# Rotary queries laid out on all 128 rows, with zeros in the other head's half, in one buffer

## The chip, the cores and the metric

The kernel runs on one NeuronCore of a Trainium2 chip, as one program. The metric is the time of one execution on the device in microseconds (us); the runs of a kernel are summed up by their median. A profile is one further execution with the hardware profiler on.

## The reference

The program computes one block of a diffusion transformer (adaptive layer norm, neighbourhood attention, convolutional feed-forward network) on 256 tokens of width 2048, and behind it a hybrid layer that adds an mLSTM branch and a branch of latent attention. All is in float32. The change lies in the latent attention, which is this:

```python
H_B = 16; D_NOPE = 128; D_ROPE = 64; D_HQK = D_NOPE + D_ROPE
...
    q_b = jnp.einsum('bsr,rn->bsn', rms_norm_2(c_q, q_lat_g), w_uq).reshape(b_sz, s_len, H_B, D_HQK)
    kv_b = jnp.einsum('bsr,rn->bsn', rms_norm_2(c_kv, kv_lat_g), w_ukv).reshape(b_sz, s_len, H_B, D_NOPE + D_VB)
    k_nope, v_b = jnp.split(kv_b, [D_NOPE], axis=-1)
    k_b = jnp.concatenate([k_nope, jnp.broadcast_to(k_r[:, :, None, :], (b_sz, s_len, H_B, D_ROPE))], axis=-1)
    q_b = rms_norm_2(q_b, q_norm_g)
    k_b = rms_norm_2(k_b, k_norm_g)
    q_b = jnp.concatenate([q_b[..., :D_NOPE], apply_rope(q_b[..., D_NOPE:], cos, sin)], axis=-1)
    k_b = jnp.concatenate([k_b[..., :D_NOPE], apply_rope(k_b[..., D_NOPE:], cos, sin)], axis=-1)
    o_b = causal_attention(q_b, k_b, v_b).reshape(b_sz, s_len, D_B)
```

So a head's query has 192 numbers, 128 plain ones and 64 that are rotated by the position; the score is the product over all 192, and 256 queries meet 256 keys under a causal mask.

## The kernel before, in words

Float32 precision comes from pairs: every operand is split into a high part (rounded to the matmul's input type, by ScalarE, ACT) and a low part (the rest, by VectorE, DVE), and a product is made of three matmuls, high by high, high by low and low by high (`mm3`), or of two where the two parts of one operand lie side by side. Weights come from HBM in tiles `raw` of 1 MB, are split into `whi` and `wlo`, and are multiplied at once. A Python planner writes the instructions out: it keeps an estimate of each engine's time, a heap of things that become due (`spawn`, `at`, `yield`), rings of buffers (`Ring`; `get` waits, in the planner, until a buffer is back), and the eight banks of PSUM. The order on each engine is the order in which the planner emits; each engine then works its list in order.

The latent attention comes after the mLSTM branch, 2 heads (a group g) at a time, 8 groups. `mla_begin` sets up the buffers. `mla_units(g)` multiplies the latents (`latkv`, `latq`) with the group's weights; `mla_q` and `mla_k` normalise and rotate the result, turn it with TensorE (PE) transposes (from `bsq`, `bx`, `bkt`) and split it: `bq` and `bk` hold the 128 plain rows, `bqr` and `bkr` the rotary ones. In `bqr` and `bkr` the 64 rotary numbers of the group's first head are rows 0 to 63, those of the second head rows 64 to 127. `mla_attn(h)` makes the scores of head h: for each block of 128 queries (t = 0, 1) three matmuls of `bk,bq` over 128 rows and three of `bkr,bqr` over the head's 64 rows, into the same bank; 128 keys for t = 0 and 256 for t = 1. So a head has 12 score matmuls, and within them the number of rows goes 128, 64, 128, 64. Behind them come mask and softmax (tile `bp`), three transposes of `bp`, the split into `bpt`, and the product with the values (`bpt,bv`, 6 matmuls over 128 rows: three with 256 columns, three with 128). Between these PE has the matmuls of the gate projection `mla_z` (`h,whi` and `h,wlo`, with 512 and 256 columns) and the next group's `latkv` and `latq`. In the rows every matmul stands under the line of `mm` (L257), a transpose under L266, and all DVE and ACT work under L152, so that names tell them apart.

Of the kernel before, what the change touches and what calls it, by code (L numbers as in the profile page):

```python
# [13 lines left out]
F32R = mybir.dt.float32r  # L14
# [520 lines left out]
def col(c):  # L535
    return slice(c * 128, (c + 1) * 128)
# [18 lines left out]
class Model(Kern):  # L555
# [1189 lines left out]
    def mla_begin(self):  # L1745
        self.need(lambda: self.y_stashed == 4)
        self.L.pop("ya")
        self.R.pop("y")
        self.sgring = Ring(self, self.L.push("sgb"), "sgb", [128, 256], F32, 8)
        p = self.R.push("obf")  # L1750
        self.obF = p.tile([128, KD, 256], F32, name="obF")
        p = self.R.push("mla")
        self.lat = {n: p.tile([128, 2, 4, 256], F32R, name="lat" + n) for n in ("q", "kv")}
        self.lat_ready = set()
        self.qring = Ring(self, p, "bq", [128, 2, 512], F32R, 2)
        self.kring = Ring(self, p, "bk", [128, 2, 512], F32R, 2)
        self.qrring = Ring(self, p, "bqr", [128, 2, 256], F32R, 2)
        self.krring = Ring(self, p, "bkr", [128, 2, 256], F32R, 2)
        self.v_left = {}
        self.vring = Ring(self, p, "bv", [128, 2, 2, 256], F32R, 2)  # L1760
        self.zring = Ring(self, p, "bz", [128, 256], F32, 6)
        self.sqring = Ring(self, p, "bsq", [128, 2, 2, 192], F32, 2)
        self.ktring = Ring(self, p, "bkt", [128, 768], F32, 1)
        self.xring = Ring(self, p, "bx", [128, 2, 2, 64], F32, 3)
        self.pring = Ring(self, p, "bp", [128, 384], F32, 2)
        self.ptring = Ring(self, p, "bpt", [128, 2, 384], F32R, 2)
        self.q, self.k, self.v, self.qr, self.kr, self.rq, self.zb = {}, {}, {}, {}, {}, {}, {}
        self.b_ready, self.ob_ready = {}, set()
        self.need(lambda: self.kr_ready)
# [10 lines left out]
    def mla_q(self, g, banks):  # L1780


        self.rq[g] = self.ccring.get()
        c = self.rq[g][0]
        x, xi = self.sqring.get()
        y, yi = self.xring.get()
        z, zi = self.xring.get()
        for t in range(2):
            o = banks[t].t[:, 0:384].rearrange("p (h c) -> p h c", h=2)
            for j in range(2):  # L1790
                self.act(y.rearrange("p t h c -> p (t h c)")[:, 0:192], o[:, j], AF.Square,
                         accum_out=c[:, 12 + 2 * t + j:13 + 2 * t + j])
            self.A.copy(out=x[:, t], in_=o)
            banks[t].free()
        yield
        yield from self.rotate(y, x[:, :, :, 128:192], z, "q", 2)
        yield from self.rsqrt(c[:, 0:4], c[:, 12:16], 192, c[:, 4:12], sign=-1.0)
        self.xring.put(zi)
        yield
        b, b2 = self.bank(), self.bank()  # L1800
        for t in range(2):
            for j in range(2):
                self.tr(b.t[:, 256 * j + 128 * t:256 * j + 128 * t + 128], x[:, t, j, 0:128])
            self.tr(b2.t[:, col(t)], y[:, t].rearrange("p h c -> p (h c)"))
        self.sqring.put(xi)
        self.xring.put(yi)
        yield 0.2
        d, di = self.qring.get()
        r, ri = self.qrring.get()
        self.q[g], self.qr[g] = (d, di), (r, ri)  # L1810
        self.act(d[:, 0], b.t, AF.Copy, scale=self.bqn)
        self.A.copy(out=r[:, 0], in_=b2.t[:, 0:256])
        yield
        self.stt(d[:, 1], b.t, self.bqn, d[:, 0].bitcast(F32), ALU.mult, ALU.subtract)
        b.free()
        self.V.tensor_sub(out=r[:, 1], in0=b2.t[:, 0:256], in1=r[:, 0])
        b2.free()
        self.mla_go(g)

# [90 lines left out]

    def mla_attn(self, h):
        g, j = h // 2, h % 2
        half, cj = slice(64 * j, 64 * j + 64), 256 * j
        q, k, qr, kr, r = self.q[g][0], self.k[g][0], self.qr[g][0], self.kr[g][0], self.rq[g][0]
        b = self.bank()
        for t in range(2):
            o = b.t[:, 0:128] if t == 0 else b.t[:, 128:384]
            qs, ks = slice(cj + 128 * t, cj + 128 * t + 128), slice(cj, cj + 128 * (t + 1))
            self.mm3(o, q[:, 0, qs], q[:, 1, qs], k[:, 0, ks], k[:, 1, ks], True, False)
            qs, ks = col(t), slice(0, 128 * (t + 1))  # L1920
            self.mm3(o, qr[half, 0, qs], qr[half, 1, qs], kr[half, 0, ks], kr[half, 1, ks], False, True)
        self.b_left[g] = self.b_left.get(g, 2) - 1
        if not self.b_left[g]:
            self.qring.put(self.q.pop(g)[1])
            self.kring.put(self.k.pop(g)[1])
            self.qrring.put(self.qr.pop(g)[1])
            self.krring.put(self.kr.pop(g)[1])
        yield 0.2
        p, pi = self.pring.get()
        s, si = self.ccring.get()  # L1930
        tri = self.con("tri0")
        V = self.V
        for t in range(2):
            c = slice(0, 128) if t == 0 else slice(128, 384)

            V.tensor_tensor_reduce(out=b.t[:, c], in0=b.t[:, c], in1=tri[:, 128:256] if t == 0 else tri,
                                   scale=r[:, 2 * t + j:2 * t + j + 1], scalar=3e38, op0=ALU.add, op1=ALU.min,
                                   accum_out=s[:, t:t + 1])
        yield
        for t in range(2):  # L1940
            c = slice(0, 128) if t == 0 else slice(128, 384)
            self.act(p[:, c], b.t[:, c], AF.Exp, scale=-1.0, bias=s[:, t:t + 1], accum_out=s[:, 2 + t:3 + t])
        b.free()
        self.rq_left[g] = self.rq_left.get(g, 2) - 1
        if not self.rq_left[g]:
            self.ccring.put(self.rq.pop(g)[1])
        yield
        V.reciprocal(out=s[:, 4:6], in_=s[:, 2:4])
        for t in range(2):
            c = slice(0, 128) if t == 0 else slice(128, 384)  # L1950
            V.tensor_scalar(out=p[:, c], in0=p[:, c], scalar1=s[:, 4 + t:5 + t], scalar2=None, op0=ALU.mult)
        self.ccring.put(si)
        yield
        b = self.bank()
        for c in range(3):
            self.tr(b.t[:, col(c)], p[:, col(c)])
        self.pring.put(pi)
        yield 0.2
        pt, pti = self.ptring.get()
        self.A.copy(out=pt[:, 0], in_=b.t[:, 0:384])  # L1960
        yield
        self.V.tensor_sub(out=pt[:, 1], in0=b.t[:, 0:384], in1=pt[:, 0])
        b.free()
        yield
        self.need(lambda: h in self.zb)
        b = self.bank()
        v = self.v[g][0]
        c = col(j)
        self.mm3(b.t[:, 0:256], v[:, 0, 0, c], v[:, 1, 0, c], pt[:, 0, 0:256], pt[:, 1, 0:256], True, False)
        self.mm3(b.t[:, 128:256], v[:, 0, 1, c], v[:, 1, 1, c], pt[:, 0, 256:384], pt[:, 1, 256:384], False, True)  # L1970
        self.ptring.put(pti)
        self.v_left[g] = self.v_left.get(g, 2) - 1
        if not self.v_left[g]:
            self.vring.put(self.v.pop(g)[1])
        yield 0.2
        z, zi = self.zb.pop(h)
        self.tt(self.obF[:, h], b.t[:, 0:256], z, ALU.mult)
        b.free()
        self.zring.put(zi)
        self.ob_ready.add(h)  # L1980
# [222 lines left out]
```

## Time and profile before

| | |
|---|---|
| median of 3 runs | 2597.22 us (2588.12, 2597.22, 2597.39) |
| the profiled execution | 2589.92 us, of which span 2588.1 us |
| PE busy | 2530.4 us, 98% of the span |
| DVE, ACT busy | 71%, 55% of the span |
| mean granted PE clock | 0.993 of full speed |
| latent attention, first and last score matmul | 2138.6 us, 2337.7 us |

The span runs from the first to the last instruction of the core. The granted clock is the share of TensorE's full 2.4 GHz that was let through; it has two levels in the trace, 1.0 and 0.5.

### The profile page before, as it was taken

To read this page: it belongs to the slowest core of one execution; us is meant where nothing else is said; L and a number is where in the kernel's file an instruction comes from. 1 tells how busy PE (TensorE), PEld (TensorE's weight loads), DVE (VectorE), ACT (ScalarE), POOL (GpSimd) and SP (SyncE) were. 2 spreads that over 40 slices of the span, in tenths; PEclk is the share of its full clock that TensorE was granted. 3 is DMA by queue.
4 is the path that set the end of the run, shared out by engine and by line. 5 is a ranking of instruction groups with operands and counts; after the bars stand their busy time and mean duration, and the time that the engine had idled before them with its cause. 6 is when DMAs were issued, how large, how long until landed. Compare 5 with 4: busy or idle time off the path is not lost.

```text
span 2588.1 us, 37928 instructions
## 1 busy us (share of the span) xinstructions
PE 2530.4 (98%) x14694; PEld 2198.0 (85%) x14694; DVE 1842.5 (71%) x2995; ACT 1418.7 (55%) x2585; POOL 241.4 (9%) x263
## 2 busy tenths in 40 slices
PE   4999999999989999999999999999999999999999
PEld 2788888888978888888888888888888888888888
DVE  7988777776688887887555567677665576677664
ACT  5664444445555555555444557666554467776442
POOL 5422111211110000000000140000000000000000
PEclk8999999999999999999999999999999999999999
DMA  7887677665656666665565654554555643345554
GB/s 271 293 257 227 218 221 218 212 219 166 215 183 226 232 219 231 228 227 199 202 210 207 204 172 174 179 188 155 179 203 188 212 171 135 123 143 204 199 208 155
DMA packets 82533, 522.19 MB, mean 202 GB/s; under 512 B 9233, under 2 KB 15377, under 8 KB 23857
## 3 DMA queue, kind: packets, MB, share of 16 engines
q1 hardware_dynamic: 76656, 501.88, 55.6%
q0 software_dynamic: 5696, 17.90, 3.9%
q8 instruction: 115, 1.88, 0.3%
q14 instruction: 66, 0.53, 0.1%
HBM read 511.35 MB, written 8.39 MB: 201 GB/s over the span
## 4 chain that ended last, share of the span: by engine, by line
PE 92%; DVE 4%; ACT 2%; DMA 1%; issue 1%; SPq 0%; DVEq 0%; ACTq 0%
PE bank L257 90%; PE bank L266 2%; DVE wlo L152 2%; DVE acc L152 1%; ACT whi L152 0%; DMA raw<-in_na_w_qkv_dram 0%; ACT L150 0%; DVE hL L152 0%; DMA nx<-in_ctxT_dram 0%; DMA raw<-in_w_ada_dram 0%; SPq L734 0%; DVE gb L152 0%; DVE mct L152 0%; ACT o L152 0%; ACT kx L152 0%
## 5 line engine op out<-in xcount | busy, mean ns | idle before, releaser
L152 DVE TENSOR_TENSOR wlo<-raw,whi 128x1024 fp32r<-128x1024 f32 (+3 forms) x822 | 983.3, 1208 | 234.5 <-ACT whi L152 229.7
L152 ACT CAST whi<-raw 128x1024 fp32r<-128x1024 f32 (+3 forms) x822 | 830.3, 1021 | 421.3 <-PE bank L257 284.6
L257 PE MATMUL bank<-h,whi 128*128 128x512 f32 (+1 forms) x1696 | 595.4, 395 | 0.0
L257 PE MATMUL bank<-hf,whi 128*128 128x512 f32 x1376 | 484.8, 397 | 2.4 <-DVE hf L152 2.4
L257 PE MATMUL bank<-h,wlo 128*128 128x256 f32 x1680 | 471.7, 281 | 0.0
L257 PE MATMUL bank<-hf,wlo 128*128 128x256 f32 x1376 | 386.9, 281 | 0.0
L257 PEld LDWEIGHTS bank<-h,whi 128*128 128x128 f32 x1696 | 318.4, 188 | 71.3 <-issue 0.4
L257 PEld LDWEIGHTS bank<-h,wlo 128*128 128x128 f32 x1680 | 318.8, 190 | 0.5 <-DVE wlo L152 0.3
L257 PEld LDWEIGHTS bank<-hf,whi 128*128 128x128 f32 x1376 | 259.1, 188 | 64.0 <-DVE hf L152 3.5
L257 PE MATMUL bank<-whi,hH 128*128 128x512 f32 (+1 forms) x832 | 287.8, 346 | 0.0
L257 PE MATMUL bank<-whi,hL 128*128 128x512 f32 (+1 forms) x832 | 284.3, 342 | 2.2 <-DVE hL L152 2.2
L257 PE MATMUL bank<-wlo,hH 128*128 128x512 f32 (+1 forms) x832 | 284.2, 342 | 1.2 <-DVE wlo L152 1.2
L257 PEld LDWEIGHTS bank<-hf,wlo 128*128 128x128 f32 x1376 | 261.3, 190 | 0.0
L257 PE MATMUL bank<-hid,whi 128*128 128x512 f32 x688 | 238.6, 391 | 0.0
L152 DVE SCALAR_TENSOR_TENSOR acc<-raw,cs,acc 128x512 f32<-128x512 f32 x240 | 188.0, 783 | 9.0 <-DMA raw<-in_w_ada_dram 2.1
L257 PE MATMUL bank<-hid,wlo 128*128 128x256 f32 x688 | 192.6, 280 | 0.0
L257 PEld LDWEIGHTS bank<-whi,hL 128*128 128x128 f32 x832 | 158.1, 190 | 20.5 <-DVE hL L152 2.4
L257 PEld LDWEIGHTS bank<-wlo,hH 128*128 128x128 f32 x832 | 158.3, 190 | 18.0 <-DVE wlo L152 1.8
L257 PEld LDWEIGHTS bank<-whi,hH 128*128 128x128 f32 x832 | 158.2, 190 | 16.6
L257 PEld LDWEIGHTS bank<-hid,whi 128*128 128x128 f32 x688 | 128.7, 187 | 28.2
L152 ACT COPY fold<-bank 128x256 f32<-128x256 f32 x118 | 43.8, 373 | 157.8 <-PE bank L257 155.5
L257 PEld LDWEIGHTS bank<-hid,wlo 128*128 128x128 f32 x688 | 130.0, 189 | 0.0
(334 smaller groups left out, 3699.5 us busy)
## 6 DMA issues: line engine op xcount, KB each, us to landing
raw<-in_w_in_dram SPq DMA_DIRECT2D x120, 1024.0 KB, 4.9
raw<-in_w_ada_dram SPq DMA_DIRECT2D x86, 1024.0 KB, 5.1
raw<-in_ffn_w_up_dram SPq DMA_DIRECT2D x86, 1024.0 KB, 4.9
raw<-in_na_w_qkv_dram SPq DMA_DIRECT2D x42, 1024.0 KB, 4.9
raw<-in_ffn_w_down_dram SPq DMA_DIRECT2D x40, 1024.0 KB, 4.9
raw<-in_na_w_o_dram SPq DMA_DIRECT2D x16, 1024.0 KB, 5.2
raw<-in_w_a_dram SPq DMA_DIRECT2D x16, 1024.0 KB, 5.0
raw<-in_w_b_dram SPq DMA_DIRECT2D x16, 1024.0 KB, 5.0
```

Of the source, the lines that this page charges most:

```text
L152: r = f(*a, **kw)
L257: self.T.matmul(out, lhsT, rhs, start=start, stop=stop)
L266: self.T.transpose(out, in_, self.con("id"))
```

## The change

`bqr` gets an axis for the head of the group: the tile of head j holds that head's 64 rotary rows in their half and zeros in the other half. The score matmul of the rotary part then takes all 128 rows of `bqr` and of `bkr`; the other head's keys are multiplied by the zeros. There is one such buffer instead of two of half the size, and its zero halves are written once, in `mla_begin`. The copy and the subtraction that fill `bqr` become two instructions each, one per half.

```diff
-        self.qrring = Ring(self, p, "bqr", [128, 2, 256], F32R, 2)
+        self.qrring = Ring(self, p, "bqr", [128, 2, 2, 256], F32R, 1)
+
+        zero = self.con("tri0")[:, 0:128].unsqueeze(1).to_broadcast([128, 4, 128])
+        for j in range(2):
+            o = slice(64 - 64 * j, 128 - 64 * j)
+            self.V.tensor_copy(out=self.qrring.tiles[0][o, j].rearrange("p a (b c) -> p (a b) c", b=2), in_=zero[o])
...
-        self.A.copy(out=r[:, 0], in_=b2.t[:, 0:256])
+        for j in range(2):
+            o = slice(64 * j, 64 * j + 64)
+            self.A.copy(out=r[o, j, 0], in_=b2.t[o, 0:256])
...
-        self.V.tensor_sub(out=r[:, 1], in0=b2.t[:, 0:256], in1=r[:, 0])
+        for j in range(2):
+            o = slice(64 * j, 64 * j + 64)
+            self.V.tensor_sub(out=r[o, j, 1], in0=b2.t[o, 0:256], in1=r[o, j, 0])
...
-            self.mm3(o, qr[half, 0, qs], qr[half, 1, qs], kr[half, 0, ks], kr[half, 1, ks], False, True)
+            self.mm3(o, qr[:, j, 0, qs], qr[:, j, 1, qs], kr[:, 0, ks], kr[:, 1, ks], False, True)
```

PE has as many instructions as before. The added DVE and ACT instructions move the planner's estimates, and so the order from `mla_begin` on. On DVE, at the end of the mLSTM branch's output projection (`y`), the two zero copies come in ahead of the next weight splits:

```order
 L152 TENSOR_TENSOR y<-bank_18545,y 128x256
 L152 TENSOR_TENSOR y<-y,sga_13558 128x256
-L152 TENSOR_TENSOR wlo<-raw,whi 128x1024 x3
-L152 TENSOR_TENSOR obF<-bank_18696,obF 128x256
+L152 CAST bqr_18674<-cons 64x512 x2
+L152 TENSOR_TENSOR wlo<-raw,whi 128x1024 x3
+L152 TENSOR_TENSOR obF<-bank_18697,obF 128x256
```

Nothing else moves there; the `obF` row differs only in the number of its bank. On PE, at the scores of the first group, before (two heads, one behind the other, and then the gate projection):

```order
L257 MATMUL bank_19618<-bk_18672,bq_18670 128x128 x3
L257 MATMUL bank_19618<-bkr_18676,bqr_18674 128x128 x3
L257 MATMUL bank_19618<-bk_18672,bq_18670 128x256 x3
L257 MATMUL bank_19618<-bkr_18676,bqr_18674 128x256 x3
L257 MATMUL bank_19637<-bk_18672,bq_18670 128x128 x3
L257 MATMUL bank_19637<-bkr_18676,bqr_18674 128x128 x3
L257 MATMUL bank_19637<-bk_18672,bq_18670 128x256 x3
L257 MATMUL bank_19637<-bkr_18676,bqr_18674 128x256 x3
```

and with the change:

```order
L257 MATMUL bank_19621<-bkr_18677,bqr_18674 128x256 x3
L257 MATMUL bank_19640<-h_11582,whi 128x512
L257 MATMUL bank_19640<-h_11582,wlo 128x256
...
L257 MATMUL bank_19640<-h_11582,whi 128x512
L257 MATMUL bank_19640<-h_11582,wlo 128x256
L257 MATMUL bank_19661<-bk_18672,bq_18670 128x128 x3
```

Eight matmuls of the gate projection now stand between the two heads. (128x128 and 128x256 are the shape of what is written; the number of rows that are summed over doesn't stand in these rows.) Two heads stood back to back in four of the eight groups before, and do in three now. On PE at the first group's value product, before:

```order
L266 MATMUL bank_19777<-cons,bp_18692 128x128 x3
L266 MATMUL bank_19784<-cons,bp_18693 128x128 x3
L257 MATMUL bank_19809<-bpt_18694,bv_18678 128x256 x3
L257 MATMUL bank_19809<-bpt_18694,bv_18678 128x128 x3
L266 MATMUL bank_19816<-cons,bsq_18687 128x128 x2
```

and with the change:

```order
L266 MATMUL bank_19776<-cons,bp_18693 128x128 x3
L266 MATMUL bank_19782<-cons,bkt_18689 128x128 x2
L266 MATMUL bank_19783<-cons,bkt_18689 128x128
L266 MATMUL bank_19782<-cons,bkt_18689 128x128 x2
L266 MATMUL bank_19783<-cons,bkt_18689 128x128
L266 MATMUL bank_19794<-cons,bp_18694 128x128 x3
L266 MATMUL bank_19805<-cons,bsq_18688 128x128 x2
L266 MATMUL bank_19806<-cons,bx_18692 128x128
L266 MATMUL bank_19805<-cons,bsq_18688 128x128 x2
L266 MATMUL bank_19806<-cons,bx_18692 128x128
L257 MATMUL bank_19825<-bpt_18695,bv_18679 128x256 x3
```

The transposes of the first head's `bp` stood three matmuls ahead of its value product, and stand fifteen ahead now.

## Rows read from the trace of the kernel before

**Rows 1.** The page: engines' busy time; the chain that ended last.
```profile
PE 2530.4 (98%) x14694; PEld 2198.0 (85%) x14694; DVE 1842.5 (71%) x2995; ACT 1418.7 (55%) x2585; POOL 241.4 (9%) x263
...
PE 92%; DVE 4%; ACT 2%; DMA 1%; issue 1%; SPq 0%; DVEq 0%; ACTq 0%
```
**Rows 2.** Windows: start:end, length; busy per engine; PEclk; DMA share, GB/s.
```profile
2090.00:2370.00 280.00, 277.24 (x1591) 242.62 (x1591) 196.65 (x476) 200.84 (x504) 10.09 (x18) 0.99 0.40 140
```
**Rows 3.** Timeline of PE, a head's scores: start us, us, what, [idle before].
```profile
2332.92 0.28 PE L257 MATMUL bank<-h,wlo 128*128 128x256 f32 x1
2333.04 0.45 PE L257 MATMUL bank<-bk,bq 128*128 128x128 f32 x3
2333.41 0.55 PE L257 MATMUL bank<-bkr,bqr 64*128 64x128 f32 x3
2333.89 0.62 PE L257 MATMUL bank<-bk,bq 128*128 128x256 f32 x3
2334.44 0.61 PE L257 MATMUL bank<-bkr,bqr 64*128 64x256 f32 x3
2334.98 0.90 PE L257 MATMUL bank<-bpt,bv 128*128 128x256 f32 x6
2335.72 0.50 PE L257 MATMUL bank<-bk,bq 128*128 128x128 f32 x3
```
**Rows 4.** Timeline of PE, a value product with no change of rows around it.
```profile
2354.61 0.80 PE L257 MATMUL bank<-bpt,bv 128*128 128x256 f32 x6
2355.25 0.45 PE L257 MATMUL bank<-h,whi 128*128 128x512 f32 x1
```
**Rows 5.** Timeline of PE, matmuls over 8 rows in the mLSTM branch.
```profile
1566.07 0.28 PE L257 MATMUL bank<-h,wlo 128*128 128x256 f32 x1
1566.28 0.69 PE L257 MATMUL bank<-gb,cons 8*128 8x256 f32 x2
```
**Rows 6.** Windows: behind groups 0 and 2, and at the scores of group 4.
```profile
2142.84:2146.00 3.16, 3.16 (x11) 2.68 (x11) 2.94 (x9) 2.40 (x12) 1.85 (x2) 0.51 0.00 0
...
2204.14:2207.40 3.26, 3.26 (x11) 2.77 (x11) 3.10 (x17) 2.26 (x8) 0.00 (x0) 0.50 0.64 196
2255.20:2259.20 4.00, 4.00 (x25) 3.20 (x24) 0.97 (x4) 3.97 (x7) 0.00 (x0) 1.00 0.64 201
```
**Rows 7.** Timeline of PE at the value product of the first group.
```profile
2156.30 0.82 PE L266 MATMUL bank<-cons,bp 128*128 128x128 f32 x6
2157.78 0.38 PE L257 MATMUL bank<-bpt,bv 128*128 128x256 f32 x1 [0.66 <-ACT bpt L152]
2158.72 0.79 PE L257 MATMUL bank<-bpt,bv 128*128 128x256 f32 x5 [0.56 <-DVE bpt L152]
```
**Rows 8.** The same view at the third group.
```profile
2220.15 1.60 PE L257 MATMUL bank<-bpt,bv 128*128 128x256 f32 x12 [1.18 <-DVE bk L152]
```
**Rows 9.** Instructions on tile bqr: ns min/median/max, first and last start, shapes.
```profile
L152 ACT CAST bqr<-bank x8: 362/366/400, 2132.5 to 2327.8; 128x256 fp32r<-128x256 f32 x8
L152 DVE TENSOR_TENSOR bqr<-bank,bqr x8: 411/415/415, 2133.3 to 2329.2; 128x256 fp32r<-128x256 f32 x8
```
**Rows 10.** Groups of DVE by shape: 512 columns out of SBUF.
```profile
L152 DVE TENSOR_TENSOR wlo<-raw,whi 128x512 fp32r<-128x512 f32 x32 | 26.1, 846 | 11.6 <-ACT whi L152 11.5
...
L152 DVE TENSOR_SCALAR acc<-raw,cs 128x512 f32<-128x512 f32 x16 | 7.9, 491 | 1.4 <-PE bank L266 1.0 <-DMA raw<-in_w_ada_dram 0.4
```
**Rows 11.** Timeline of DVE where the zero copies come in.
```profile
2039.54 1.22 DVE L152 TENSOR_TENSOR wlo<-raw,whi 128x1024 fp32r<-128x1024 f32 x1
2041.44 1.23 DVE L152 TENSOR_TENSOR wlo<-raw,whi 128x1024 fp32r<-128x1024 f32 x1 [0.69 <-ACT whi L152]
2044.27 1.22 DVE L152 TENSOR_TENSOR wlo<-raw,whi 128x1024 fp32r<-128x1024 f32 x1 [1.60 <-ACT whi L152]
```
**Rows 12.** Timelines of PE (group 6's last scores) and ACT (group 7's bqr).
```profile
2315.64 0.62 PE L257 MATMUL bank<-bkr,bqr 64*128 64x256 f32 x3
...
2327.84 0.37 ACT L152 CAST bqr<-bank 128x256 fp32r<-128x256 f32 x1
```

More of the change, by code (lines that the diff above doesn't have):

```diff
@@ L1912, in mla_attn @@
         g, j = h // 2, h % 2
-        half, cj = slice(64 * j, 64 * j + 64), 256 * j
+        cj = 256 * j
         q, k, qr, kr, r = self.q[g][0], self.k[g][0], self.qr[g][0], self.kr[g][0], self.rq[g][0]
```

## The prediction

> **What bounds the kernel now.** I read the page first. PE is busy for 98% of the span and makes up 92% of the chain that ended last [rows 1], so what PE doesn't have to do comes off the end nearly whole, and work on DVE or ACT costs only where PE comes to wait for it. The change touches one stage, so I went to its window next: from 2090 to 2370 us PE is busy for 277.2 of 280 us, DVE for 196.7 and ACT for 200.8 [rows 2]. This stage is bound by PE too, and the other two have some 80 us of room in it.
>
> A busy share doesn't say whether PE runs at its pace, so I read its timeline at one head's scores. The four groups of three matmuls begin at 2333.04, 2333.41, 2333.89 and 2334.44, and what follows at 2334.98 [rows 3]: 1.94 us for 12 matmuls. The value product is the yardstick: six matmuls of the same widths, all over 128 rows, begin at 2354.61 and the next work at 2355.25 [rows 4], 0.64 us, so 12 would take 1.28. Right behind the scores the same product needs 0.74 (2334.98 to 2335.72) [rows 3], 0.10 more. The lost time stands at the places where the number of rows changes: the group that runs from 2333.41 to 2333.89 has three matmuls of 128 columns and takes 0.48, while a `h,wlo` matmul of 256 columns takes 0.12 to the start of the next [rows 3]. One other place of the program shows the same: ahead of a matmul over 8 rows, a `h,wlo` takes 0.21 instead of 0.12 [rows 5].
>
> Last I looked at the clock, by windows. It stands at 0.51 from 2142.84 to 2146.00 and at 0.50 from 2204.14 to 2207.40, right behind two pairs of heads that stand back to back; at another such pair, from 2255.2 to 2259.2, it stays at 1.00 [rows 6]. So a dense run of these interrupted matmuls came ahead of both falls (PE had matmuls all the time), but not every such run is followed by one.
>
> **The change part by part.**
>
> *The changes of rows go.* A head's scores cost 1.94 + 0.10 = 2.04 us now. With 128 rows throughout there is no change left, within or behind them; PE's instructions are the same in number and width. The 12 then take 1.28 by the value product; the upper bound is 12 x 0.12 = 1.44, if each takes as long as a `h,wlo`. I take 1.35: six of the scores of 128 columns come in a row, where the value product has three between wider ones. That saves 0.69 a head, 11.0 us for 16 heads (9.6 to 12.2). No row shows a zero half being multiplied; the time of a matmul in these rows goes by its columns, so I give the zeros no price.
>
> *The clock.* At half clock a stretch does half its work: 3.16 x 0.49 + 3.26 x 0.50 = 3.2 us lost in the profiled execution [rows 6]. With the interruptions gone I expect both falls to go: a gain of 3.2, bounds 0 (they stay, or move to another place) and 3.2.
>
> *The order.* At the first group PE waited for the split of `bpt` twice: from the start of the six transposes at 2156.30 (0.66 of work) to 2157.78, and from there to 2158.72 [rows 7], 1.6 us of waiting in all, since only three transposes stood between a head's transposes and its value product. Fifteen stand there now, 12 x 0.11 = 1.3 us more, so I take 1.3 of the 1.6 as won. The other wait like it, 1.18 us for DVE's `bk` [rows 8], I leave as it is; other places may get worse. Bounds 3 won, 2 lost.
>
> *Added on ACT and DVE.* In each group ACT has one copy more and DVE one subtraction more. Their row count halves and their columns stay 256, and the rows on `bqr` give 0.37 and 0.41 us for 256 columns [rows 9]; I take the same for half the rows, 0.78 a group, 6.2 us over the kernel if none of it is covered. The cover is the 80 us of room [rows 2] and PE's other matmuls between a group's splits and its scores. PE was late by such work in two groups of eight [rows 7, 8], and one of those is moved apart; so I count one group, 0.8. What is queued behind them on DVE and ACT are weight splits, which are made some sub-tiles ahead of PE.
>
> *The zero copies.* Two DVE copies of 512 columns. Nothing of that shape with 64 rows stands in the trace; the nearest rows are 491 ns (one input) and 846 ns (two inputs) [rows 10], so 1.0 to 1.7 us together, nearer to the first. They stand on DVE ahead of the splits at 2041.44 and 2044.27, which wait 0.69 and 1.60 us for ACT anyhow [rows 11]; that takes the delay up. Price 0; 1.7 if the cover were gone.
>
> *One buffer.* Group g + 1 may fill `bqr` only when the scores of group g are read. The closest pair is the last: group 6's scores end at about 2316.2 and group 7's copy starts at 2327.84 [rows 12], 11.6 us later. Price 0.
>
> **The sum.** 11.0 + 3.2 + 1.3 - 0.8 = 14.7 us off. The profiled execution took 2589.92 (span 2588.1), so it becomes 2575.2. The median of the three runs is 7.3 us above it, near two of them, and nothing in the profile says what those two spend more; I carry the saving over to the median: 2597.2 - 14.7 = 2582.5.
>
> **The rivals.**
>
> 1. *The gaps go, the clock doesn't follow.* The window at 2255.2 [rows 6] shows that such a run need not pull the clock down; in the runs that are timed there may have been fewer falls, or new ones come elsewhere. Then 11.0 to 11.5 us are won: 2586. 0.25.
> 2. *DVE and ACT are not covered.* For it: two of eight groups waited on them [rows 7, 8], and PE, being quicker, leaves them less time. All 6.2 us on the path: 14.7 + 0.8 - 6.2 = 9.3 won, 2588. 0.12.
> 3. *The number of rows is not what causes the gaps*, but for instance the change from one pair of tiles to another. Against it: `bpt,bv` behind `h,wlo` starts without a gap, and the 8 rows show one [rows 4, 5]. Then nothing is won but the order's share: 2596 to 2598. 0.06.
> 4. *Half-row matmuls ran beside others*, and the full rows take that away. In the trace, three of 64 rows and 128 columns take 0.48 us, more than three full ones, with their starts one behind the other [rows 3]; nothing is run beside them. If half of a head's rotary time (0.48 + 0.54) were hidden now, 0.51 x 16 = 8.2 us would be lost from the sum: 2591. 0.02. The Trainium skill has a rule to this end ("TensorE: Matmul & The Clock Gate", Part 3: Packing small matmuls): small-K operands laid into distinct row groups run concurrently, so that slices of 64 rows would be kept, not padded. By that rule the sum would be 6.5 instead of 14.7; the trace doesn't agree here, since neighbouring rotary matmuls sit in the same rows and a full-row matmul always follows.
> 5. *Slower: the one buffer holds back the next group.* If the planner or ACT had to wait for a group's scores before the next group's `bqr`, each of 7 groups would add the way from that copy to its scores (2327.84 [rows 12] to 2333.04 [rows 3], 5.2 us): 36 us, less 14.7 won, 2619. It decides once the 11.6 us of slack are used up, and the changed order keeps groups about as far apart. 0.03.
>
> **How the numbers follow.** The forecast has 0.52: 14.7 us, by its own bounds 12 to 17.5. The predicted time is 2582.5. Its lower end is the profiled execution's level (2575.2) and a good order (3 won, not 1.3), and a clean pitch of 1.28: 2571. The upper end takes in rivals 1 and 2: 2590. Outside lie rivals 3 to 5 and what else the level of the runs does. 0.5% of the time, 13 us, is about what a measurement of this kernel can tell from no change. The forecast lies just above it, so about nine tenths of its chance and a little of rival 1 count as faster: 0.52. Rivals 1 to 4 and the rest are no change by that bound: 0.45. Slower: 0.03.
>
> **What would show it.** In the changed profile a head's 12 score matmuls should take 1.3 to 1.4 us instead of 1.94, in groups of 0.33 to 0.37, with 128 rows in `bkr,bqr`; what follows should start at its usual pace; no window at half clock should stand between 2130 and 2340; the waits of PE in that stage should be no more than the 2.8 us of [rows 2]. If the groups still take 0.48 and 0.54, the step on the rows is wrong; if they take 0.35 and the time is the same, PE waits elsewhere, and the waits will name it.

## The result and the profile after

The changed kernel takes 2579.94 us (median of 6 runs, 2577.96 to 2584.01) against 2596.09 us before (6 runs, 2588.12 to 2597.84); the medians are 16 us apart. The ratio taken over the runs is 0.9946, with a 95% interval of 0.993 to 0.9962: 0.54% or 14 us less, 10 to 18 by the interval. 14.7 us and 2582.5 were predicted. In a second comparison on another occasion the ratio was 0.9956 (0.9942 to 0.997).

The page of the changed kernel, engines' busy time and the chain, to be laid beside [rows 1]:

```profile
PE 2520.4 (98%) x14694; PEld 2191.8 (85%) x14694; DVE 1846.4 (72%) x3005; ACT 1421.1 (55%) x2593; POOL 239.6 (9%) x263
...
PE 92%; DVE 4%; ACT 2%; DMA 1%; issue 1%; SPq 0%; DVEq 0%; ACTq 0%
```

PE is busy for the same share of the span, with as many instructions, but for 10 us less in all. Where they went, the timeline of PE at a head's scores shows, with the same neighbours as in [rows 3]:

```profile
2322.03 0.28 PE L257 MATMUL bank<-h,wlo 128*128 128x256 f32 x1
2322.15 0.45 PE L257 MATMUL bank<-bk,bq 128*128 128x128 f32 x3
2322.43 0.50 PE L257 MATMUL bank<-bkr,bqr 128*128 128x128 f32 x3
2322.77 0.57 PE L257 MATMUL bank<-bk,bq 128*128 128x256 f32 x3
2323.17 0.52 PE L257 MATMUL bank<-bkr,bqr 128*128 128x256 f32 x3
2323.53 0.80 PE L257 MATMUL bank<-bpt,bv 128*128 128x256 f32 x6
2324.17 0.50 PE L257 MATMUL bank<-bk,bq 128*128 128x128 f32 x3
```

The 12 score matmuls run from 2322.15 to 2323.53: 1.38 us, where they took 1.94. The value product behind them takes 0.64 (to 2324.17) instead of 0.74, so the 0.10 behind the scores is gone too. All rotary matmuls are over 128 rows now, and the three of 128 columns take 0.34 instead of 0.48.

The windows of the changed kernel, first the stretch of [rows 2], then that with all the scores; the last three numbers are the granted clock, the DMA share and GB/s:

```profile
2090.00:2370.00 280.00, 279.27 (x1684) 250.34 (x1683) 215.02 (x509) 212.34 (x527) 11.50 (x19) 1.00 0.46 159
...
2130.00:2340.00 210.00, 209.64 (x1297) 190.27 (x1295) 162.03 (x406) 164.71 (x425) 8.69 (x14) 1.00 0.43 147
```

The clock stays at 1.00 (in the kernel before, 0.98 over the second stretch), and PE is idle for 0.7 us of the 280 instead of 2.8. What is left of the waiting stands in the timeline at the first group's value product, to be laid beside [rows 7]:

```profile
2161.24 1.17 PE L257 MATMUL bank<-bpt,bv 128*128 128x256 f32 x7
2162.75 0.68 PE L257 MATMUL bank<-bpt,bv 128*128 128x256 f32 x4 [0.34 <-DVE bpt L152]
```

The added work stands on the tile `bqr` (ns min/median/max, first and last start), beside [rows 9]:

```profile
L152 ACT CAST bqr<-bank x16: 352/364/369, 2139.1 to 2315.1; 64x256 fp32r<-64x256 f32 x16
L152 DVE TENSOR_TENSOR bqr<-bank,bqr x16: 404/417/428, 2139.9 to 2317.3; 64x256 fp32r<-64x256 f32 x16
L152 DVE CAST bqr<-cons x2: 420/422/425, 2046.2 to 2046.7; 64x512 fp32r<-64x512 f32 x2
```

Half the rows take the full time: 0.364 and 0.417 us for 64 rows, 0.366 and 0.415 for 128. The zero copies take 0.42 us each, below the nearest row, 0.49 [rows 10].

For the comparisons I measure the stage by two starts that the tiles' rows show: from the first score matmul (`bank<-bk,bq`) to the first matmul on `ob`, before which all heads must be done. Before, these are 2138.7 and 2362.4, 223.7 us apart. With the change:

```profile
L257 PE MATMUL bank<-bk,bq x96: 220/278/335, 2145.3 to 2325.1; 128*128 128x128 f32 x48, 128*128 128x256 f32 x48
...
L257 PE MATMUL bank<-ob,whi x256: 391/391/468, 2353.1 to 2485.9; 128*128 128x512 f32 x128
```

2353.1 - 2145.3 = 207.8, 16 us less. The profiled executions differ by only 9.4 us (2589.92 and 2580.54), because the changed one reached its first score matmul 6.6 us later (2145.3 against 2138.7). Nearly all of that isn't the change: 5.8 us of it were lost by the end of the down projection, ahead of the first changed instruction; the last section shows how.

### The profile page after: what moved, and what is told of

Same layout as the page of the kernel before. It is cut to its first block, busy times and chain, and to the rows that moved or that the text cites. A ratio compares the mean times of both kernels' runs of the same rounds, so it can differ in the third digit from the quotient of the medians.

```text
span 2578.8 us, 37954 instructions
## 1 busy us (share of the span) xinstructions
PE 2520.4 (98%) x14694; PEld 2191.8 (85%) x14694; DVE 1846.4 (72%) x3005; ACT 1421.1 (55%) x2593; POOL 239.6 (9%) x263
## 4 chain that ended last, share of the span: by engine, by line
PE 92%; DVE 4%; ACT 2%; DMA 1%; issue 1%; SPq 0%; DVEq 0%; ACTq 0%
PE bank L257 90%; PE bank L266 2%; DVE wlo L152 2%; DVE acc L152 1%; DMA raw<-in_na_w_qkv_dram 0%; ACT whi L152 0%; ACT L150 0%; DVE hL L152 0%; DMA nx<-in_ctxT_dram 0%; DMA raw<-in_w_ada_dram 0%; SPq L734 0%; DVE hf L152 0%; DVE gb L152 0%; DVE mct L152 0%; ACT o L152 0%
```

## The experiments

All in one table; the stage is measured as above in the profiled execution, the clock is the mean granted one over a run, averaged over the runs. The kernel before has 0.9937 in 38 runs. "Changed, again" and "the same again" run a kernel a second time.

| kernel | stage, us | median, us | ratio to before, interval | clock |
|---|---|---|---|---|
| before | 223.7 | 2593.7 to 2596.1 | | 0.9937 |
| changed | 207.8 | 2579.94 | 0.9946 (0.9930 to 0.9962) | 0.9953 |
| changed, again | 207.7 | 2582.49 | 0.9956 (0.9942 to 0.9970) | 0.9950 |
| rows back to 64 | 218.5 | 2592.18 | 0.9991 (0.9981 to 1.0002) | 0.9940 |
| order of before kept | 210.1 | 2585.45 | 0.9956 (0.9943 to 0.9970) | 0.9944 |
| grouped, two changes of rows | 216.3 | 2587.37 | 0.9965 (0.9953 to 0.9977) | 0.9950 |
| in turn, twelve changes | 267.1 | 2636.04 | 1.0155 (1.0141 to 1.0169) | 0.9835 |
| fills twice | 207.7 | 2581.88 | 0.9955 (0.9941 to 0.9968) | 0.9950 |
| 8-row matmul over 128 rows | 207.7 | 2580.62 | 0.9943 (0.9928 to 0.9959) | 0.9952 |
| the same again | 207.7 | 2578.10 | 0.9936 (0.9919 to 0.9953) | 0.9952 |
| halves side by side | 208.3 | 2585.03 | 0.9962 (0.9948 to 0.9976) | 0.9948 |
| side by side, other order, 8 rows | 211.0 | 2580.11 | 0.9937 (0.9918 to 0.9956) | 0.9948 |

**Rows back to 64.** The changed kernel, with the rotary matmuls cut to their head's half. Order, buffers and fills stay.

```diff
-            self.mm3(o, qr[:, j, 0, qs], qr[:, j, 1, qs], kr[:, 0, ks], kr[:, 1, ks], False, True)
+            self.mm3(o, qr[half, j, 0, qs], qr[half, j, 1, qs], kr[half, 0, ks], kr[half, 1, ks], False, True)
```

Expected:

> The changed kernel with one thing undone: the rotary score matmuls read only their head's 64 rows again, out of the new tile. The order on all engines, the zero copies, the doubled fills and the one buffer stay. Measure of the stage: from the first score matmul to the first matmul on ob, 223.7 us before and 207.8 with the change. Theory (the changes of row count cost 0.69 us a head, and the clock falls behind some pairs of heads): a head's scores take 1.94 us again, the stage 219 to 223 us, the whole 11 to 15 us more than the changed kernel (2591 to 2595). Rival (something else in the change, order or buffers, made the gain): the stage stays at 208 us and the whole within 3 us of the changed kernel, about 2580.

The timeline of PE at its first scores behind `latkv`:

```profile
2168.74 0.44 PE L257 MATMUL bank<-bk,bq 128*128 128x128 f32 x3
2169.11 0.55 PE L257 MATMUL bank<-bkr,bqr 64*128 64x128 f32 x3
2169.59 0.62 PE L257 MATMUL bank<-bk,bq 128*128 128x256 f32 x3
2170.14 0.61 PE L257 MATMUL bank<-bkr,bqr 64*128 64x256 f32 x3
2170.68 0.55 PE L257 MATMUL bank<-bk,bq 128*128 128x128 f32 x3
```

2168.74 to 2170.68 is 1.94 us again, and the stage is 10.7 us longer than in the changed kernel, with nothing else altered. That is the price of 64 changes of row count (four a head, 16 heads), 0.17 us each, and the rival falls. In the profiled execution no window at half clock lies in the stage, so the 10.7 us hold none of that; the mean clock over 11 runs, 0.9940, lies near the 0.9937 of the kernel before, so it probably fell in other executions, but no trace shows where.

**Order of before kept.** The changed kernel, with the added instructions issued past the planner's clock, so that PE's order is that of before.

```diff
-            self.A.copy(out=r[o, j, 0], in_=b2.t[o, 0:256])
+            (self.A if j == 0 else self.A.e).copy(out=r[o, j, 0], in_=b2.t[o, 0:256])
...
-            self.V.tensor_sub(out=r[o, j, 1], in0=b2.t[o, 0:256], in1=r[o, j, 0])
+            (self.V if j == 0 else self.V.e).tensor_sub(out=r[o, j, 1], in0=b2.t[o, 0:256], in1=r[o, j, 0])
```

(The zero copies likewise.) Expected:

> The changed kernel, with the added DVE and ACT instructions hidden from the planner, so that PE's order is that of the kernel before. Theory (the order gave some 1.3 to 2 us by moving transposes of bp away from the value product, the row counts gave 11 and the clock 3): the two waits for bpt and the one for bk are there again, 2.5 to 3 us of waiting on PE in the stage, no window at half clock, the stage takes 209 to 211 us, the whole 2580 to 2584. Rival (the new order is the main thing): the stage takes 216 us or more. Rival (back-to-back pairs pull the clock down whatever their rows): one or two windows at half clock behind groups 0 and 2, 1.7 us each.

PE's waits from 2140 to 2360 (who waited for whom, us in total, times, longest):

```profile
PE bank L257 <- DVE bk L152: 1.2, 1, 1.2
PE bank L257 <- ACT bpt L152: 0.7, 1, 0.7
PE bank L257 <- DVE bpt L152: 0.6, 1, 0.6
```

These are the waits of [rows 7, 8] again, 2.5 us, where the changed kernel has 0.3. The stage takes 2.3 us more than in the changed kernel: that is what the order gave. The back-to-back pairs of before stand there again, over full rows, and no window in the stage is at half clock in this execution. The mean clock over the five runs is 0.9944, though, below the 0.9950 to 0.9953 of the changed kernel, and the median, 2585.45 us, lies above the 2580 to 2584 that I expected.

**Grouped.** The kernel before, with a head's two blocks over 128 rows first, then its two blocks over 64 rows: two changes of rows a head.

```diff
-            self.mm3(o, q[:, 0, qs], q[:, 1, qs], k[:, 0, ks], k[:, 1, ks], True, False)
+            self.mm3(o, q[:, 0, qs], q[:, 1, qs], k[:, 0, ks], k[:, 1, ks], t == 0, False)
+        for t in range(2):
+            o = b.t[:, 0:128] if t == 0 else b.t[:, 128:384]
             qs, ks = col(t), slice(0, 128 * (t + 1))
-            self.mm3(o, qr[half, 0, qs], qr[half, 1, qs], kr[half, 0, ks], kr[half, 1, ks], False, True)
+            self.mm3(o, qr[half, 0, qs], qr[half, 1, qs], kr[half, 0, ks], kr[half, 1, ks], False, t == 1)
```

Expected:

> The kernel before, with a head's scores in another order: both blocks of queries over 128 rows first, then both over 64 rows. Two changes of row count a head instead of four, the same matmuls. Theory (each change of rows costs about 0.17 us): a head takes about 1.6 us and 0.10 behind it, the stage 5.5 us less than before (218), or up to 3.4 less than that if the clock no longer falls; the whole 2586 to 2591. Rival (64-row matmuls are slow in themselves): a head takes 1.94 us still, the stage 223.7.

The timeline of PE at the first group, two heads one behind the other:

```profile
2145.20 0.85 PE L257 MATMUL bank<-bk,bq 128*128 128x128 f32 x6
2145.98 0.95 PE L257 MATMUL bank<-bkr,bqr 64*128 64x128 f32 x6
2146.86 0.95 PE L257 MATMUL bank<-bk,bq 128*128 128x128 f32 x6
```

The first head takes 1.66 us (2145.20 to 2146.86), near the 1.6 expected. The stage takes 216.3 us, 7.4 less than before. No half clock lies in it, which is 3.2 to 3.4 of that; the other 4 us are 32 changes fewer, 0.13 each. The number of 64-row matmuls is that of before, so these 4 us are the price of the changes and not of 64-row matmuls as such.

**In turn.** The same dose upwards: a 128-row matmul and a 64-row one by turns, twelve changes a head.

```diff
-            self.mm3(o, q[:, 0, qs], q[:, 1, qs], k[:, 0, ks], k[:, 1, ks], True, False)
...
-            self.mm3(o, qr[half, 0, qs], qr[half, 1, qs], kr[half, 0, ks], kr[half, 1, ks], False, True)
+            for n, (x, y) in enumerate(((0, 0), (0, 1), (1, 0))):
+                self.mm(o, q[:, x, qs], k[:, y, ks], n == 0, False)
+                self.mm(o, qr[half, x, qs2], kr[half, y, ks2], False, n == 2)
```

Expected:

> The kernel before, with a matmul over 128 rows and one over 64 rows in turn: 12 changes of row count a head instead of four, the same matmuls. Theory (0.17 us a change): a head takes 1.94 + 8 x 0.17 = 3.3 us, the stage 22 us more than before (246), the whole 2618, more if the clock falls more often. Rival (64-row matmuls are slow in themselves, wherever they stand): the stage stays at 223.7 and the whole at 2596.

PE at its first head, first matmul and the one behind the head, and the window of its stage:

```profile
2143.15 0.22 PE L257 MATMUL bank<-bk,bq 128*128 128x128 f32 x1
...
2146.46 0.33 PE L257 MATMUL bank<-bk,bq 128*128 128x128 f32 x1
...
2143.00:2410.00 267.00, 264.62 (x1285) 219.28 (x1284) 156.20 (x390) 158.98 (x406) 7.08 (x14) 0.89 0.33 114
```

The first head, still at full clock, takes 3.31 us where 3.3 was expected: 1.37 more than 1.94 for eight more changes, 0.17 each. The stage is 43 us longer than before. A clock of 0.89 over 267 us is 29 us lost, against some 3 before; the remaining 17 us are 128 changes more, 0.14 each. PE is busy for 264.6 of 267 us here and its waits are those of before (`bk` 1.2 us, `bpt` 1.3), so no added waiting came with the clock's fall: only the changes of rows were added. (The busy time takes in what the changes cost; of a head's 3.31 us, 1.38 would do over full rows.) My number, 246, had left the clock open ("more if the clock falls more often"); it fell far more often than I thought.

**Fills twice.** The changed kernel, with each copy and subtraction that fills `bqr` issued twice.

```diff
             self.A.copy(out=r[o, j, 0], in_=b2.t[o, 0:256])
+            self.A.e.copy(out=r[o, j, 0], in_=b2.t[o, 0:256])
...
             self.V.tensor_sub(out=r[o, j, 1], in0=b2.t[o, 0:256], in1=r[o, j, 0])
+            self.V.e.tensor_sub(out=r[o, j, 1], in0=b2.t[o, 0:256], in1=r[o, j, 0])
```

Expected:

> The changed kernel with every copy and every subtraction that fills the rotary queries done twice, the second time over the same place and hidden from the planner: 0.78 us more on ACT and 0.83 on DVE in each group, PE's order as in the changed kernel. Theory (this work is covered by PE's other matmuls): the stage, from the first score matmul to the first on ob, takes 207.7 to 208.7 us as in the changed kernel, and the whole stays within 2 us of it. Rival (work on ACT and DVE ahead of the scores is on the path): 0.8 to 1.6 us a group, the stage takes 214 to 221 us, the whole 6 to 13 us more.

The stage takes 207.7 us (2143.3 to 2351.0): twice the extra work costs nothing either, and PE's wait for `bpt` is the same 0.3 us. The median, 2581.88, lies within 2 us of the changed kernel's on the same occasion (2582.49).

**8-row matmul over 128 rows.** The changed kernel, with the same idea at the place of [rows 5].

```diff
-        for nm in ("gi", "gz", "ga", "gb", "gc", "gone"):
+        for nm in ("gi", "gz", "ga", "gc", "gone"):
...
+        self.gb128 = p.tile([128, 256], F32, name="gb")
+        self.gb = self.gb128[0:8]
+        self.V.memset(self.gb128, 0.0)
...
-        self.mm(bm.t[:, 0:256], self.cons[0:8, i0 + h:i0 + h + 1].to_broadcast([8, 128]), self.gb, True, True)
+        self.mm(bm.t[:, 0:256], self.cons[:, i0 + h:i0 + h + 1].to_broadcast([128, 128]), self.gb128, True, True)
```

Expected:

> The changed kernel, with the same done at another place: the mLSTM branch's matmul over 8 rows (gate row of a head spread over all rows), 8 times, is made over 128 rows, with zeros below the 8 rows. Theory (each change of rows costs PE time): the eight places, which take 0.21 + 0.32 + 0.30 us each now, take 0.12 for each of the three, 0.47 less, 3.8 us off the whole: 2576. Rival (8-row matmuls are slow for their type, not for their rows): nothing, 2580.

The timeline of PE at the first of the eight places, in the changed kernel:

```profile
1572.70 0.28 PE L257 MATMUL bank<-h,wlo 128*128 128x256 f32 x1
1572.90 0.69 PE L257 MATMUL bank<-gb,cons 8*128 8x256 f32 x2
1573.53 0.90 PE L257 MATMUL bank<-mq,mk 128*128 128x256 f32 x6
```

and in this one:

```profile
1573.23 0.28 PE L257 MATMUL bank<-h,wlo 128*128 128x256 f32 x1
1573.35 0.59 PE L257 MATMUL bank<-gb,cons 128*128 128x256 f32 x2
1573.59 0.88 PE L257 MATMUL bank<-mq,mk 128*128 128x256 f32 x5
```

From `h,wlo` to `mq,mk` 0.83 us became 0.36, so 0.47 less, at each of the eight places: 3.8 us, as expected there. The whole was expected at 2576 and came out at 2580.62, which can't be told apart from the changed kernel: the intervals of the ratios overlap. The stretch around the eight places can be: from the last matmul of the down projection to the first score it is 670.3 to 671.2 us in the three profiled executions with this place changed, and 673.5 to 674.6 in three of the changed kernel without it (as it is, again, fills twice), some 3.4 us less. The same kernel was run a second time:

> The changed kernel with the 8-row matmul over 128 rows once more, beside the run above. Theory: the stage takes 207.7 us again; the whole 2573 to 2582, with 3 to 4 us less than the changed kernel at the same pace of the long streams.

The stage takes 207.7 us and the whole 2578.10, both as expected.

**Halves side by side.** The kernel before, with both heads of a group scored in one go: their 128-row matmuls first, then the 64-row ones by turns from rows 0 to 63 and from rows 64 to 127.

```diff
+        for j in range(2):
+            for t in range(2):
...
+                self.mm3(o, q[:, 0, qs], q[:, 1, qs], k[:, 0, ks], k[:, 1, ks], t == 0, False)
+        for t in range(2):
...
+            for n, (x, y) in enumerate(((0, 0), (0, 1), (1, 0))):
+                for j in range(2):
...
+                    half = slice(64 * j, 64 * j + 64)
+                    self.mm(o, qr[half, x, qs], kr[half, y, ks], False, t == 1 and n == 2)
```

Expected:

> The kernel before, with both heads of a group scored together: the 128-row matmuls of both, then the 64-row matmuls in turn, one in rows 0 to 63, the next in rows 64 to 127, into two banks. Two changes of row count a group instead of eight. Theory (neighbours in different halves don't run at once by more than their starts, as the rows of before show for neighbours in the same half): 12 rotary matmuls of a group take 1.4 us as full ones would, the changes cost 0.3 to 0.4 a group, the two heads take about 3.1 us together instead of 3.9, the stage 214 us or less, the whole 2584 to 2588. Rival (halves run at once): 12 rotary matmuls take 0.7 us, the two heads 2.3 to 2.4 us, less than the 2.76 with zeros, and the stage is 3 us shorter than the changed kernel's.

The timeline of PE at the first group:

```profile
2145.04 1.54 PE L257 MATMUL bank<-bk,bq 128*128 128x128 f32 x12
2146.51 0.96 PE L257 MATMUL bank<-bkr,bqr 64*128 64x128 f32 x12
2147.40 0.50 PE L257 MATMUL bank<-h,whi 128*128 128x512 f32 x1
```

Twelve 64-row matmuls take 0.89 us (2146.51 to 2147.40) with the changes of rows included, where twelve full ones take 2 x (0.34 + 0.36) = 1.40. My theory said 1.4; the rival was right, halves run at once. The twelve pass 2304 columns (six times 128 and six times 256), and 0.89 us at 2.4 GHz are 2136 cycles: more columns than cycles, which matmuls one behind the other at one column a cycle could not do. Two heads take 2.36 us, 0.40 less than with zeros (2 x 1.38); of that the change behind them takes 0.11 back (the next matmul starts at 2147.74, after 0.34 us instead of 0.23). The stage isn't shorter for it, 208.3 us: PE waits here for `bk` (1.2 us), `obF` (1.0) and `bpt` (0.4), 2.6 us in all against 0.3. That part of the rival, a stage 3 us shorter, didn't come.

**Side by side, other order.** The same, with the planner's delays before the second head's softmax and before the value product raised to 2.5 and 2 us, and the 8-row place as above.

> The two heads of a group scored together with their 64-row matmuls side by side, as in the run before; the planner starts the second head's softmax 2.5 us after the first's and puts at least 2 us more between the split of bpt and the value product; and the mLSTM branch's 8-row matmul is made over 128 rows. Theory (halves run at once, 0.4 us less a group than with zeros; the waits of 3 to 4 us of that run came from the order alone): the waits for bpt go, the stage from the first score matmul to the first on ob takes 204.5 to 206 us against 207.7 with the change, the whole is 2 to 6 us less than the changed kernel: 2575 to 2579. Rival (waiting moves on to other banks and splits): the stage takes 207 us or more, and only the 8-row place gains, about 3 us.

Its waits from 2140 to 2360:

```profile
PE bank L257 <- DVE bk L152: 2.0, 2, 1.2
PE bank L257 <- DVE wlo L152: 1.6, 2, 1.2
PE bank L266 <- DVE obF L152: 1.1, 1, 1.1
```

The waits for `bpt` went and others came, 5 us in all (the three longest are shown); the stage takes 211.0. The rival held. By time it stands level with the other version with the 8-row place changed (0.9937 and 0.9936): I found no version that is clearly quicker than the changed kernel.

**Changed, again**, for comparison beside these:

> The changed kernel once more, beside the three above on the same chip, for comparison. Theory: its stage takes 207.7 us again and no window at half clock lies behind the scores; the whole lies between 2577 and 2584 by the level at which the long matmul streams of the other stages run in that execution.

Its stage takes 207.7 us, without a window at half clock, and the whole 2582.49.

## Why the prediction was right

*What bounds the kernel.* That time taken from PE's work comes off the end held: the stage lost 16 us, and what follows it takes as long as before (225.7 us from the first matmul on `ob` to the end in both profiled executions).

*The changes of rows* were put at 11.0 us. A head's share is 2.04 - 1.38 = 0.66, or 10.6 for 16, and rows set back to 64 cost 10.7. The clean scores take 1.38 where I took 1.35, in groups of 0.28 to 0.40 and not all between 0.33 and 0.37. The runs with two and twelve changes move with the number of changes, 0.13 to 0.17 us each. The Trainium skill ("TensorEngine Tiling (Array Packing)", Tiling Modes) says that changing the tiling mode drains TensorE, and that changing only the tile doesn't; these runs agree with both: changes between 64 and 128 rows cost 0.13 to 0.17 us each, and with the halves side by side eleven changes of tile and two of rows fit into twelve matmuls' 0.89 us, where at 0.17 each the changes of tile alone would take 1.9.

*The clock* was put at 3.2 us. In the profiled executions that is what it gave: both falls are gone. Over the runs, 0.9937 against 0.9952 (12 runs of the changed kernel) is 0.0015 x 2590 = 3.9 us, but this mean takes in stretches outside the stage, where the two profiles differ too (0.91 before and 0.99 after, from 20 to 40 us). Whether the rows or the order keep the clock up is not shown. In one profiled execution each, neither the old order over full rows nor the new order over 64 rows has a window at half clock in the stage, and over the runs both lie between the two kernels, at 0.9944 (5 runs) and 0.9940 (11 runs). What is shown is that many more changes pull it down: 0.89 over the stage with twelve a head.

*The order* was put at 1.3 us and gave 2.3, the one term that was clearly off. I had left the wait for `bk` [rows 8] as it was, and it went too: the profile after shows 0.3 us of waiting where [rows 7, 8] show 2.4 in PE's own rows. The waits for `bpt`, on which I had counted, gave 0.9 of it, and the one for `bk`, which I hadn't forecast, 1.2.

*The added work* was put at 0.8 us and costs nothing; twice of it costs nothing. The room of 80 us on DVE and ACT [rows 2] was cover enough. The zero copies cost 0.86 us on DVE and nothing that shows: from the last matmul of the down projection to the first score it is 673.8 us before, and 673.5 to 674.6 in three executions with them. The one buffer held nothing back: the closest pair is still the last, where group 7's first copy starts at 2314.8, some 9.3 us after the end of group 6's scores (about 2305.5), and 11.6 were there before.

*The sum*: 10.7 + 3.2 + 2.3 = 16.2 against the 16.0 measured in the stage, and 14.7 predicted; the 14 us by the ratio of the runs, 10 to 18, can't tell the two apart. The median came out 2.6 us under the predicted one. The lower end of the predicted range, 2571, doesn't follow from its terms: 2575.2 less 1.7 for the order and 1.1 for the pitch is 2572.4. Of the rivals, the first doesn't hold in the profiled execution, where the clock stays at 1.00, nor by the median (2579.9 against its 2586); the second and fifth fall to the fills twice and the stage, the third to the rows set back. The fourth was right about the chip and wrong about this kernel: half-row matmuls do run at once if neighbours lie in different halves, but before the change neighbours lay in the same half, so nothing was lost by giving it up.

*Where I was lucky.* I carried the profile's saving over to the median without knowing what made single runs differ by 9 us. Any two single executions of the first comparison would have shown a gain, but of anything from 4 to 20 us. And half of the order's 2.3 us came from a wait that I had expected to stay.

## What to carry to other kernels

Look at a short matmul stretch for the pitch of its instructions, not for PE's busy share: PE was 98% busy and still lost 0.13 to 0.17 us at each change of the number of rows. Where matmuls over fewer rows stand between full ones, either pad them with zeros, or group them, or lay neighbours in different halves, and count the changes that are left (a head took 1.94 us, and 1.38, 1.66 and 1.18 in these three ways). If instructions that are added on other engines move a planner's order, measure the order by itself; here it was a seventh of the gain.

## What I had not expected of the hardware

**Halves run at once.** Twelve matmuls over 64 rows took 0.89 us, by turns in the two halves, against 1.40 for twelve over 128 rows. The rule that spoke against the change (the Trainium skill, "TensorE: Matmul & The Clock Gate", Part 3: Packing small matmuls) is borne out by this run.

**One stream, two paces.** The long streams of a 512-column and a 256-column matmul by turns ran at one of two paces, with the same order, at full clock. The rows of the same 688 matmuls of the down projection, upstream of the change, in the kernel before:

```profile
L257 PE MATMUL bank<-hid,whi x688: 391/391/391, 1226.8 to 1464.9; 128*128 128x512 f32 x172
```

and in the changed kernel:

```profile
L257 PE MATMUL bank<-hid,whi x688: 395/398/403, 1227.9 to 1470.7; 128*128 128x512 f32 x172
```

238.1 us and 242.8 us, 2.0% apart, at a granted clock of 1.00 in both. All twelve profiled executions took one or the other, three of them 238.1 or 238.2 us and nine 242.7 or 242.8, and in this stream the minimum, median and maximum tell which: all 391, or 395 to 404. It isn't tied to the kernel: the one with the 8-row place changed took 242.7 in one execution and 238.2 in the other, and the last stream of the program (`ob` and what follows) took 225.7 us in the profiled executions of the kernel before and the changed one, and 230.0 in the profiled execution of the changed kernel's second run. This is where the changed kernel's profile lost most of the 6.6 us before its first score, and it is large enough to make the 9 us between single runs of one kernel; what chooses the pace is open, I tried nothing on it.

**The clock falls in a busy engine.** With twelve changes of rows a head it stood at 0.89 over 267 us in which PE was busy, by the profile, for 264.6.
